# Retention's gates moved behind its keys, values and queries, and its states made among the gates

## The chip, the core and the metric

The kernel runs on one core of a Trainium2 chip. The engines named are PE (TensorE, matmul), DVE (VectorE), ACT (ScalarE), POOL (GpSimd) and SP (SyncE, which here only issues DMAs). The metric is the device time of one execution in microseconds. Before the change three timed runs took 4200.82, 4213.84 and 4215.55 us. One further execution was profiled.

## The reference, cut to what matters

Two blocks of a network follow each other on 1024 tokens of width 1024 (the second block has 256 context tokens as well). The change touches the even layer of the second block, whose mixers are retention and RWKV-7. Both are computed in both directions, for tokens and for context.

```python
u_l = h_l @ w_in                      # also u_c = h_c @ w_in for the context
q, k, v = ret_qkv(u)                  # 8 heads of 64; q and k are rotated for the tokens
gate = silu(u[..., E_RZ:E_WZ])        # and a second gate of 512 columns for RWKV

def retention_scan(q, k, v, log_g, s0):          # chunks of 128 tokens
    scores = einsum('bhncd,bhnsd->bhncs', qc, kc) * dmat       # decay matrix inside a chunk
    y_intra = einsum('bhncs,bhnse->bhnce', scores, vc)
    kv = einsum('bhnsd,bhnse->nbhde', kc * k_decay, vc)
    s_fin, s_prev = lax.scan(lambda s, kv_n: (g_chunk * s + kv_n, s), s0, kv)
    y_cross = einsum('bhncd,nbhde->bhnce', qc * q_decay, s_prev)
    return y_intra + y_cross, s_fin

# forward: context, then tokens from the context's last state; backward: the same on flipped sequences
ret_o = head_rms(ret_fwd + ret_bwd) * gate
y = concat([ret_o, rw_o]) @ w_out
```

`rwkv7_scan` is a recurrence with a state of 64 x 64 for each head; the kernel computes it in chunks of 64 tokens, for which it inverts small triangular matrices.

## The kernel before, in words

The 1280 tokens are ten tiles of 128: tiles 0 to 7 are tokens, 8 and 9 the context. The normalised input lies feature-major in three blocks: block 0 (tiles 0 to 3), block 1 (tiles 4 to 7) and block 2 (the context, 256 columns). Each block and each weight is held as a high part and a low part, and a product takes three matmuls for each of eight slices of the inner dimension, 24 in all (`mm3`, lines 217 to 219). In a profile row, `pf<-whi,hhi` with 128x256 is a projection of keys, values or queries, where weights are the moving side, and `pf<-hhi,whi` is a gate, where the input is moving, with 512 columns for blocks 0 and 1 and 256 for block 2.

A scheduler sets the order of instructions on every engine when the program is built. It takes what is ready in the order of the program text and fills gaps with later work. In the text of `mixers` (line 1488) RWKV comes first and retention behind it. So retention's work serves as filler between RWKV's.

`rwkv` runs ten batches, one chunk pair of the forward and one of the backward direction in each. `prep2` (from line 1580) loads and scales the operands, `invert` (from 1655) inverts on DVE with 31 pairs of a multiply and a reduction (L1670, L1671) and sends the result through DRAM, `merge` (from 1676) reads it back (`wV<-wrd`) and begins with the matmuls of L1694, and `chain` (from 1718) carries the state from chunk to chunk.

Retention in the text before: `ret_proj` is called for block 0, 1 and 2 in turn, and each call does the keys (`rk`), values (`rv`) and queries (`rq`) of the block, six weight tiles, and then its gates (`zT`), eight weight tiles. All results go to DRAM. Block 0 is still in SBUF; blocks 1 and 2 are reloaded (L1508) into the same two buffers of `hA`. Weights are split into high and low for block 0 and read back from DRAM for the others (`whi<-wkh`, `wlo<-wkl`).

`ret_state` stands behind all projections. It loads keys and values of one tile (two buffers), scales the keys on POOL for both directions (L1367), multiplies with values for all eight heads, one matmul of 128x128 by 64 columns each (L1370), and ACT copies the halves into the state array `rS` in SBUF (L1375). Then two chains of nine steps on POOL (L1382, L1383) add up the decayed states, one direction after the other. The decay matrices `rdm` are made on ACT and POOL. `mix_tile` (line 1387) then computes one tile of both mixers' outputs, with states and decay matrices read from SBUF.

Of the kernel before, what the change touches and what calls it, by code (L numbers as in the profile page):

```python
# [10 lines left out]
F32 = mybir.dt.float32  # L11
# [28 lines left out]
class Ker:  # L40
# [995 lines left out]
    def ctx_norm(self):  # L1036
# [227 lines left out]
    def ret_proj(self, p, blocks):  # L1264
# [38 lines left out]

        wc = self.wn // KD
# [15 lines left out]
    def ret_state(self, p, pl):  # L1320
# [3 lines left out]
        lg = p.tile([P, 16], F32, name="rlg")  # L1324
# [3 lines left out]
        tc_ = p.tile([P, 8], F32, name="rtc")  # L1328
        nc.sync.dma_start(tc_, a["c_rtc"])
        qdec = p.tile([P, 8, 2], F32, name="rqdec")  # L1330
        kdec = p.tile([P, 8, 2], F32, name="rkdec")
        gch = p.tile([P, 8], F32, name="rgch")
        for dd in range(2):
            l8 = lg[:, 8 * dd:8 * dd + 8]
            nc.vector.tensor_scalar(qdec[:, :, dd], l8, tc_[:, dd:dd + 1], None, op0=OP.mult)
            nc.vector.tensor_scalar(kdec[:, :, dd], l8, tc_[:, 2 + dd:3 + dd], None, op0=OP.mult)
# [5 lines left out]
        dm = p.tile([P, 8, P], F32, name="rdm")  # L1342
        rel = pl.tile([P, 4, P], F32, name="rrel", tag="rrel", bufs=1)
        nc.sync.dma_start(rel, a["c_rrel"])
        for h in range(8):
            e2 = pl.tile([P, 2, P], F32, name="re2", tag="re2", bufs=2)
# [3 lines left out]
            nc.gpsimd.tensor_add(dm[:, h], e2[:, 0], e2[:, 1])  # L1350

        S_ = p.tile([P, 10, 8, 64], F32, name="rS")
        nc.gpsimd.memset(S_[0:64, 8], 0.0)
        nc.gpsimd.memset(S_[64:128, 9], 0.0)

        nxt = [{8: 9, 9: 0}, {9: 8, 8: 7}]
        for t in range(7):
            nxt[0][t] = t + 1
            nxt[1][t + 1] = t
        for t in [8, 9] + list(range(8)):  # L1360
            k = pl.tile([P, 8, 64], F32, name="rkl", tag="rkl", bufs=2)
            nc.sync.dma_start(k, k_d[t].rearrange("p (h d) -> p h d", d=64))
            v = pl.tile([P, 512], F32, name="rvl", tag="rvl", bufs=2)
            nc.sync.dma_start(v, v_d[t])
            kd = pl.tile([P, 8, 2, 64], F32, name="rkd", tag="rkd", bufs=2)
            for dd in range(2):
                nc.gpsimd.tensor_mul(kd[:, :, dd], k, kdec[:, :, dd:dd + 1].to_broadcast([P, 8, 64]))  # L1367
            ps = self.pf()
            for h in range(8):
                nc.tensor.matmul(ps[:, 64 * h:64 * h + 64], kd[:, h].rearrange("p a d -> p (a d)"),  # L1370
                                 v[:, 64 * h:64 * h + 64], start=True, stop=True)
            for dd in range(2):
                rows = slice(64 * dd, 64 * dd + 64)
                if t in nxt[dd]:
                    nc.scalar.copy(S_[rows, nxt[dd][t]].rearrange("p h d -> p (h d)"), ps[rows])  # L1375
        for dd, t0 in ((0, 8), (1, 9)):
            rows = slice(64 * dd, 64 * dd + 64)
            t = t0
            while t in nxt[dd]:
                n = nxt[dd][t]  # L1380
                tm = pl.tile([P, 8, 64], F32, name="rtm", tag="rtm", bufs=2)
                nc.gpsimd.tensor_mul(tm[rows], S_[rows, t], gch[rows, :, None].to_broadcast([64, 8, 64]))  # L1382
                nc.gpsimd.tensor_add(S_[rows, n], S_[rows, n], tm[rows])  # L1383
                t = n
        self.rt = qdec, dm, S_

    def mix_tile(self, p, pe, t, cat, cv):
# [3 lines left out]
        qdec, dm, S_ = self.rt  # L1391
# [1246 lines left out]
```

## Time and profile before

| what | value |
|---|---|
| timed runs, median | 4213.84 us |
| profiled execution | 4202.26 us, span 4199.8 us |
| mean granted clock of PE | 0.927 of full speed |
| PE busy | 3812.9 us (91%) |
| DVE, ACT, POOL busy | 2130.2, 1320.4, 1129.9 us |
| first and last retention projection | about 2060 us, 2806.6 us |
| last matmul of RWKV | 2926.11 us |
| mix tiles | 2931 to about 3105 us |

The granted clock says how fast PE ran in a stretch: 1.00 is its higher level, 0.50 its lower one. A busy share of PE near 100% says that its stream has work, not which of its work others wait for. For that the chain of waits is read: it follows the work that ended last back from step to step, and gives each piece to an engine and a line.

### The profile page before, as it was taken

What the parts mean: (1) busy time and instruction counts of PE and PEld (TensorE: products, weight loads), DVE (VectorE), ACT (ScalarE), POOL (GpSimd) and SP (SyncE); (2) the same over time, 40 slices, a digit from 0 to 9 for tenths busy, and PEclk for the clock granted to TensorE, in tenths of its full rate; (3) what the DMA queues carried; (4) which work ended last, traced back from release to release, by engine and by line L of the source; (5) the groups of instructions that cost most, each with busy time, mean ns of one, the idle gap of its engine ahead of it and who ended that gap; (6) DMA issues with size and microseconds to landing.
All of it is one profiled execution on the core that took longest, in us unless ns stands there. A gap on an engine that the chain in (4) does not pass through costs nothing. (4 is left out here: it accounts for less than half of the span.)

```text
span 4199.8 us, 59342 instructions
## 1 busy us (share of the span) xinstructions
PE 3812.9 (91%) x23289; PEld 3077.8 (73%) x23289; DVE 2130.2 (51%) x3284; ACT 1320.4 (31%) x2641; POOL 1129.9 (27%) x1153
## 2 busy tenths in 40 slices
PE   7999989988999999789879899887889999998997
PEld 4788877776878788667767687776567877776775
DVE  4232434447343434644337686665556427653576
ACT  4333332215312121442233333332224224332211
POOL 1110202123101011202256343236431200003674
PEclk8999979998999999988989999876899999998998
DMA  5321227573141413333477655653754644324465
GB/s 201 123 100 67 98 84 264 189 263 118 50 148 63 147 50 129 126 125 122 138 229 221 187 161 173 206 157 99 234 188 142 225 134 125 102 70 152 165 203 193
DMA packets 453574, 627.03 MB, mean 149 GB/s; under 512 B 142577, under 2 KB 302499, under 8 KB 447152
## 3 DMA queue, kind: packets, MB, share of 16 engines
q1 hardware_dynamic: 402816, 421.50, 31.1%
q0 software_dynamic: 50480, 201.75, 14.5%
q8 instruction: 184, 3.01, 0.3%
q14 instruction: 94, 0.77, 0.1%
HBM read 427.27 MB, written 195.19 MB: 148 GB/s over the span
## 5 line engine op out<-in xcount | busy, mean ns | idle before, releaser
L217 PE MATMUL p<-hhi,whi 128*128 128x512 f32 x1056 | 415.8, 394 | 5.9 <-DVE hf L389 5.8
L218 PE MATMUL p<-hlo,whi 128*128 128x512 f32 x1056 | 414.3, 392 | 4.3 <-DVE hlo L391 4.3
L219 PE MATMUL p<-hhi,wlo 128*128 128x512 f32 x1056 | 413.8, 392 | 0.0
L217 PE MATMUL pf<-whi,hhi 128*128 128x512 f32 (+1 forms) x992 | 359.0, 362 | 29.4 <-ACT rqr L1279 9.4
L218 PE MATMUL pf<-wlo,hhi 128*128 128x512 f32 (+1 forms) x992 | 352.4, 356 | 3.7 <-DVE wlo L177 3.4
L177 DVE TENSOR_TENSOR wlo<-wraw,whi 128x2048 fp32r<-128x2048 f32 (+1 forms) x103 | 212.3, 2062 | 273.8 <-ACT whi L176 267.8
L219 PE MATMUL pf<-whi,hlo 128*128 128x512 f32 (+1 forms) x992 | 349.3, 353 | 0.0
L176 ACT CAST whi<-wraw 128x2048 fp32r<-128x2048 f32 (+1 forms) x123 | 193.2, 1575 | 459.6 <-PE pt L219 174.7
L217 PE MATMUL pf<-hhi,whi 128*128 128x512 f32 (+1 forms) x640 | 252.4, 394 | 6.0 <-DVE zt L1311 2.1
L218 PE MATMUL pf<-hlo,whi 128*128 128x512 f32 (+1 forms) x640 | 252.0, 394 | 0.0
L219 PE MATMUL pf<-hhi,wlo 128*128 128x512 f32 (+1 forms) x640 | 249.4, 390 | 0.0
L217 PEld LDWEIGHTS pf<-whi,hhi 128*128 128x128 f32 x992 | 198.7, 200 | 68.2 <-issue 14.1
L217 PE MATMUL pj<-whi,hhi 128*128 128x512 f32 (+1 forms) x560 | 216.5, 389 | 26.5 <-ACT whi L176 12.1
L217 PEld LDWEIGHTS p<-hhi,whi 128*128 128x128 f32 x1056 | 200.4, 190 | 54.1 <-DVE hf L389 6.2
L218 PEld LDWEIGHTS p<-hlo,whi 128*128 128x128 f32 x1056 | 200.2, 190 | 46.3 <-DVE hlo L391 5.3
L219 PEld LDWEIGHTS p<-hhi,wlo 128*128 128x128 f32 x1056 | 200.0, 189 | 42.6 <-issue 0.8
L218 PEld LDWEIGHTS pf<-wlo,hhi 128*128 128x128 f32 x992 | 198.9, 200 | 28.9 <-issue 4.1
L219 PE MATMUL pj<-whi,hlo 128*128 128x512 f32 (+1 forms) x560 | 214.1, 383 | 3.0 <-DVE hlo L381 3.0
L218 PE MATMUL pj<-wlo,hhi 128*128 128x512 f32 (+1 forms) x560 | 215.1, 384 | 0.2 <-DVE wlo L177 0.2
L219 PEld LDWEIGHTS pf<-whi,hlo 128*128 128x128 f32 x992 | 198.5, 200 | 22.1 <-issue 1.3
L1670 DVE TENSOR_TENSOR wtm<-wT,wL 128x2 f32<-128x2 f32 (+30 forms) x310 | 145.7, 470 | 37.5 <-POOL wL L1661 28.0
L217 PEld LDWEIGHTS pf<-hhi,whi 128*128 128x128 f32 x640 | 122.9, 192 | 37.9 <-issue 6.7
(750 smaller groups left out, 8544.6 us busy)
## 6 DMA issues: line engine op xcount, KB each, us to landing
wraw<-w_in POOLq DMA_DIRECT2D x25, 1024.0 KB, 6.0
wraw<-w_ada POOLq DMA_DIRECT2D x24, 1024.0 KB, 8.5
wraw<-w_up POOLq DMA_DIRECT2D x22, 1024.0 KB, 6.0
whi<-wkh POOLq DMA_DIRECT2D x40, 512.0 KB, 5.6
wlo<-wkl POOLq DMA_DIRECT2D x40, 512.0 KB, 5.2
wraw<-ada_w POOLq DMA_DIRECT2D x32, 512.0 KB, 4.5
ox<-x SPq DMA_DIRECT2D x48, 256.0 KB
xp<-xl SPq DMA_DIRECT2D x48, 256.0 KB
```

Of the source, the lines that this page charges most:

```text
L176: nc.scalar.copy(hi[:, :n], raw[:, :n])
L177: self.we.tensor_sub(lo[:, :n], raw[:, :n], hi[:, :n].bitcast(F32))
L217: mm(out, L[0], R[0], start=first, stop=False)
L218: mm(out, L[0], R[1], start=False, stop=False)
L219: mm(out, L[1], R[0], start=False, stop=last)
L1670: nc.vector.tensor_mul(tv, T[:, r0:, i:], L[:, i:i + 1, i:].to_broadcast([P, 16 - r0, n]))
```

## The change

Three things are changed. First, keys, values and queries of all three blocks come first, and the gates of all blocks behind them, in the order of blocks 2, 1, 0. Block 2 is still in SBUF then, and blocks 1 and 0 are reloaded, so block 0 is now stored as well (line 1048). Second, the states are made step by step beside the gates: a generator does one step for each gate of a block and is run out at the end. A step takes four heads and both directions at once, the forward direction in partitions 0 to 63 and the backward one in 64 to 127, each at its own tile. Its keys and values have one buffer each; the sum with the decayed state is done by DVE from PSUM. Every state goes to DRAM. Third, the decay matrices go to DRAM too, and the mix tiles load states and matrices from there.

```diff
-        for b in (1, 2):
+        for b in range(3):
             hT = self.nT[b]
             self.nT_d[b] = [self.dr.tile(list(t.shape), F32, name=f"nTd{b}{x}") for t, x in zip(hT, "hl")]
...
+    def ret_gates(self, p, blocks):
...
         for c0 in range(0, 1024, wc):
             W = self.wcols_kept(self.kept, w, 1536 + c0, wc)
             for c in range(0, wc, P):
-                self.proj_fm(self.nT, W, c, ev_z((c0 + c) // P), blocks)
+                for b in blocks:
+                    self.proj_fm(self.nT, W, c, ev_z((c0 + c) // P), [b])
+                    yield
...
+        order = ([8, 9] + list(range(8)), [9, 8] + list(range(7, -1, -1)))
+        for g in range(2):
+            S_ = pl.tile([P, 4, 64], F32, name="rS", tag="rS", bufs=2)
+            nc.gpsimd.memset(S_, 0.0)
+            for n in range(10):
+                for dd in range(2):
+                    rows = slice(64 * dd, 64 * dd + 64)
+                    nc.sync.dma_start(self.st_d[order[dd][n]][rows, g], S_[rows].rearrange("p h d -> p (h d)"))
+                if n == 9:
+                    break
+                k = pl.tile([P, 2, 4, 64], F32, name="rkl", tag="rkl", bufs=1)
+                v = pl.tile([P, 2, 256], F32, name="rvl", tag="rvl", bufs=1)
+                for x, x_d in ((k.rearrange("p a h d -> p a (h d)"), k_d), (v, v_d)):
+                    for dd in range(2):
+                        nc.sync.dma_start(x[:, dd], x_d[order[dd][n]][:, 256 * g:256 * g + 256])
+                nc.gpsimd.tensor_mul(k, k, kdec[:, :, 4 * g:4 * g + 4, None].to_broadcast([P, 2, 4, 64]))
+                ps = self.pf()
+                for h in range(4):
+                    for dd in range(2):
+                        nc.tensor.matmul(ps[64 * dd:64 * dd + 64, 64 * h:64 * h + 64], k[:, dd, h],
+                                         v[:, dd, 64 * h:64 * h + 64], start=True, stop=True, tile_position=(0, 64 * dd))
+                tm = pl.tile([P, 4, 64], F32, name="rtm", tag="rtm", bufs=1)
+                nc.gpsimd.tensor_mul(tm, S_, gch[:, 4 * g:4 * g + 4, None].to_broadcast([P, 4, 64]))
+                S_ = pl.tile([P, 4, 64], F32, name="rS", tag="rS", bufs=2)
+                nc.vector.tensor_add(S_, tm, ps[:, :256].rearrange("p (h d) -> p h d", d=64))
+                yield
...
+            dm = pl.tile([P, P], F32, name="rdm", tag="rtm", bufs=1)
+            nc.gpsimd.tensor_add(dm, e2[:, 0], e2[:, 1])
+            nc.sync.dma_start(self.dm_d[:, h], dm)
...
+        S_ = p.tile([P, 8, 64], F32, name="rSl", tag="rSl", bufs=3)
+        nc.sync.dma_start(S_, self.st_d[t].rearrange("p g (h d) -> p (g h) d", d=64))
...
+            with self.pool("rpb") as pb:
+                self.ret_tables(pb)
+                for b in range(3):
+                    if b:
+                        block(b)
+                    self.ret_proj(pb, [b])
+
+            with self.pool("rzb") as pb, self.pool("rsl") as pl:
+                steps = self.ret_state(pl)
+                for b in (2, 1, 0):
+                    if b < 2:
+                        block(b)
+                    for _ in self.ret_gates(pb, [b]):
+                        next(steps, None)
+                self.run(steps)
```

Here `block(b)` reloads block b into the two buffers of `hA`. The order of the built programs shows what the scheduler makes of it. On PE, where RWKV ends, before: the last four groups are of `chain`, and the mix stage (`colr`, `wraw`, `rql`) follows at once.

```order
L1746 MATMUL p_20019<-wxv,wam 64x64 x8
L1753 MATMUL p_20019<-wrs,wX_1_13941 64x64 x8
L1779 MATMUL p_20019<-wS,wrr 64x64 x8
L1784 MATMUL p_20019<-wxv,wam 64x64 x8
L405 MATMUL pf<-ident,colr 128x8
L282 MATMUL pa<-wraw,cT_7260 32x512 x2
L1409 MATMUL pf<-ident,rql 128x128 x4
```

On PE at the same place after the change (lines of `chain` are 16 higher there): the last two groups of `chain` stand between gates.

```order
L219 MATMUL pf<-hhi,wlo 128x512
L217 MATMUL pf<-hhi,whi 128x512
L1795 MATMUL p_20020<-wS,wrr 64x64 x8
L1800 MATMUL p_20020<-wxv,wam 64x64 x8
L218 MATMUL pf<-hlo,whi 128x512
L219 MATMUL pf<-hhi,wlo 128x512
L217 MATMUL pf<-hhi,whi 128x512
```

Behind the last group of `chain` 98 matmuls of gates stand before the mix stage begins. Next, SP's queue at the last merges, before: the inversion is stored (`wrd`) and read back (`wV`), one load of values for the states (`rvl`) follows, and loads and stores of `chain`.

```order
L1674 DMA wrd_13966<-wT 1024x1x32 x2
L1686 DMA wV<-wrd_13966 32x8x32 x8
L1364 DMA rvl<-rv_13887 128x512
L1714 DMA wxv<-rw_vt_12036 64x4x64
L1715 DMA wxv<-rw_vt_12036 64x4x64
L1788 DMA rwy_6_13913<-wyt 128x256
L1714 DMA wxv<-rw_vt_12037 64x4x64
```

SP's queue at the last merges after the change: `rst` are the stores of states, `rvl` and `rkl` the loads of a step, `nTd0h` and `nTd0l` the reload of block 0.

```order
L1702 DMA wV<-wrd_13967 32x8x32 x3
L1804 DMA rwy_1_13919<-wyt 128x256
L1702 DMA wV<-wrd_13967 32x8x32 x5
L1730 DMA wxv<-rw_vt_12041 64x4x64
L1731 DMA wxv<-rw_vt_12041 64x4x64
L1315 DMA zT<-zt 128x512
L1359 DMA rst_22265<-rS 64x256
L1359 DMA rst_22264<-rS 64x256
L1366 DMA rvl<-rv_13888 128x256
L1366 DMA rvl<-rv_13887 128x256
L1512 DMA hhi<-nTd0h 128x4096
L1512 DMA hlo<-nTd0l 128x4096
```

Stores and loads of the states, and the reload of block 0, now stand in SP's queue between RWKV's own loads. Two loads of keys stand directly ahead of these rows, between the store of the inversion and its first read.

## Rows read from the trace of the kernel before

**Rows 1.** By stretch: length, busy PE, PEld, DVE, ACT, POOL, PEclk, DMA share, GB/s.

```profile
2236.70:2299.40 62.70, 59.26 (x618) 49.28 (x618) 50.02 (x104) 22.79 (x51) 41.73 (x54) 0.90 0.73 223
2299.40:2383.90 84.50, 72.67 (x798) 59.40 (x797) 58.95 (x117) 31.89 (x77) 32.61 (x40) 0.92 0.67 216
2383.90:2456.50 72.60, 66.15 (x798) 57.83 (x797) 54.11 (x116) 28.02 (x76) 34.62 (x65) 0.98 0.52 147
2456.50:2524.90 68.40, 63.31 (x766) 56.72 (x765) 50.30 (x110) 26.11 (x71) 28.18 (x49) 0.90 0.57 168
2524.90:2590.20 65.30, 61.05 (x670) 50.69 (x671) 52.15 (x115) 22.19 (x58) 28.02 (x52) 0.97 0.58 163
2590.20:2677.60 87.40, 74.26 (x802) 62.44 (x801) 52.47 (x114) 30.02 (x78) 21.61 (x38) 0.90 0.65 200
2677.60:2759.00 81.40, 64.29 (x779) 57.22 (x779) 49.81 (x112) 27.84 (x74) 23.36 (x41) 0.89 0.74 219
2759.00:2825.70 66.70, 60.40 (x695) 53.15 (x696) 53.96 (x122) 26.41 (x75) 26.61 (x40) 0.78 0.45 133
2825.70:2900.20 74.50, 57.29 (x541) 53.35 (x540) 50.04 (x98) 21.85 (x50) 55.70 (x60) 0.50 0.32 82
2900.20:2927.20 27.00, 19.36 (x482) 16.88 (x480) 12.62 (x22) 9.59 (x26) 14.50 (x15) 0.88 0.19 55
2927.20:2950.00 22.80, 17.02 (x123) 11.62 (x121) 7.23 (x14) 8.69 (x17) 10.41 (x11) 0.81 0.97 306
```

**Rows 2.** The chain of waits from 2236 to 2900 us, its share by line.

```profile
by line: DVE wtm L1670 11.7%; DVE wT L1671 7.6%; DMA wV<-wrd 5.8%; DMA wlt<-wam 5.2%; PE pf L217 4.9%; issue 4.7%; PE pf L218 4.5%; PE pf L219 4.3%; PE pj L1642 3.4%; DMA wrd<-wT 3.4%; DVE wam L1644 3.2%; DVE wxv L1738 2.9%; DVE wt L1772 2.
```

**Rows 3.** PE's timeline: start and length in us; two gate matmuls, five steps apart.

```profile
2352.12 0.39 PE L217 MATMUL pf<-hhi,whi 128*128 128x512 f32 x1
...
2353.28 0.39 PE L219 MATMUL pf<-hhi,wlo 128*128 128x512 f32 x1
```

**Rows 4.** Timelines at the reload of block 1: SP's issue, PE's first uses of each half.

```profile
2353.70 0.34 SPq L1508 DMA_DIRECT2D hhi<-nTd1h  x1
...
2362.48 0.36 PE L217 MATMUL pf<-whi,hhi 128*128 128x256 f32 x1
...
2371.73 0.56 PE L219 MATMUL pf<-whi,hlo 128*128 128x256 f32 x1
```

**Rows 5.** PE's timeline in the last batch of RWKV and at its end.

```profile
2905.52 0.69 PE L1784 MATMUL p<-wxv,wam 128*64 128x64 f32 x16
2906.13 0.69 PE L1701 MATMUL p<-wX,wQ 32*32 32x32 f32 x32
...
2931.04 0.24 PE L405 MATMUL pf<-ident,colr 8*128 8x8 f32 x1 [3.81 <-DMA colr<-rw_ln_b]
```

**Rows 6.** Busy time by stretch, of the states' matmuls (L1370) alone.

```profile
2806.60:2900.20 93.60, 36.96 (x160) 34.95 (x160) 0.52 0.34 88
```

**Rows 7.** Four lines of POOL and one of DVE: shortest, median, longest in ns.

```profile
L1367 POOL TENSOR_TENSOR rkd<-rkl,rkdec x20: 1040/1048/1375, 2818.4 to 2881.8; 128x512 f32<-128x512 f32 x20
L1382 POOL TENSOR_TENSOR rtm<-rS,rgch x18: 1034/1041/1324, 2813.3 to 2910.5; 64x512 f32<-64x512 f32 x18
L1383 POOL TENSOR_TENSOR rS<-rS,rtm x18: 1254/1262/1521, 2837.9 to 2911.6; 64x512 f32<-64x512 f32 x18
L1739 POOL TENSOR_TENSOR wS<-wt,wfc x38: 607/648/1049, 2261.2 to 2920.7; 128x256 f32<-128x256 f32 x38
L1772 DVE TENSOR_TENSOR wt<-p,wS x76: 403/422/430, 2259.3 to 2920.1; 64x256 f32<-64x256 f32 x76
```

**Rows 8.** Busy time by stretch, of the inversion's multiplies (L1670) alone.

```profile
2695.00:2738.00 43.00, 10.80 (x31) 1.00 0.65 202
...
2839.00:2878.00 39.00, 22.61 (x31) 0.50 0.29 88
```

**Rows 9.** Waits of SP's queue, 2806 to 2900 us: total, times, longest.

```profile
SPq L1362 <- POOL rkd L1367: 16.8, 7, 3.7
...
SPq L1364 <- PE pf L1370: 9.5, 5, 6.2
```

More of the change, by code (lines that the diff above doesn't have):

```diff
@@ L1341, in ret_state @@
         nc.vector.tensor_scalar(kdec, kdec, 0.125, None, op0=OP.mult)
-        dm = p.tile([P, 8, P], F32, name="rdm")
-        rel = pl.tile([P, 4, P], F32, name="rrel", tag="rrel", bufs=1)
+        self.st_d = [self.dr.tile([P, 2, 256], F32, name=f"rst{t}") for t in range(10)]
+        self.dm_d = self.dr.tile([P, 8, P], F32, name="rdmd")
+        order = ([8, 9] + list(range(8)), [9, 8] + list(range(7, -1, -1)))
[24 more added lines that the diff above has]
+                yield
+        rel = pl.tile([P, 4, P], F32, name="rrel", tag="rkl", bufs=1)
         nc.sync.dma_start(rel, a["c_rrel"])
         for h in range(8):
-            e2 = pl.tile([P, 2, P], F32, name="re2", tag="re2", bufs=2)
+            e2 = pl.tile([P, 2, P], F32, name="re2", tag="rS", bufs=2)
             for dd in range(2):
@@ L1349, in ret_state @@
             nc.gpsimd.tensor_mul(e2, e2, rel[:, 2:4])
[L1350 to L1385, printed above, removed]
+            dm = pl.tile([P, P], F32, name="rdm", tag="rtm", bufs=1)
+            nc.gpsimd.tensor_add(dm, e2[:, 0], e2[:, 1])
+            nc.sync.dma_start(self.dm_d[:, h], dm)
+        self.qdec = qdec
     def mix_tile(self, p, pe, t, cat, cv):
         nc = self.nc
-        qdec, dm, S_ = self.rt
+        qdec, dm = self.qdec, self.dm
         py = lambda: self.ps.tile([P, 512], F32, name="py", tag="py", bufs=2)
@@ L1430, in mix_tile @@
             nc.tensor.matmul(o, sD[:, h % 2, h // 2], v[:, 64 * h:64 * h + 64], start=True, stop=False)
-            nc.tensor.matmul(o, qdT[:, h], S_[:, t, h], start=False, stop=True)
+            nc.tensor.matmul(o, qdT[:, h], S_[:, h], start=False, stop=True)
         cols = slice(t * P, t * P + P)
@@ L1494, in mixers @@
         self.open_ps(2)
-        with self.pool("rwm") as p, self.pool("rpb") as pb:
+        with self.pool("rwm") as p:
             self.rwkv(p)
@@ L1499, in mixers, with block @@
             self.we = self.nc.gpsimd
-            self.ret_tables(pb)
             self.kept = {}
-            for b in range(3):
-                if b:
-                    n = 512 if b < 2 else 256
-                    hT = tuple(self.hA.tile([P, KD, 512], F32R, name="h" + x, tag=f"h{x}", bufs=1)[:, :, :n]
-                               for x in ("hi", "lo"))
-                    for t, src in zip(hT, self.nT_d[b]):
-                        self.nc.sync.dma_start(t.bitcast(F32), src)
-                    self.nT[b] = hT
-                self.ret_proj(pb, [b])
+            def block(b):
+                n = 512 if b < 2 else 256
+                hT = tuple(self.hA.tile([P, KD, 512], F32R, name="h" + x, tag=f"h{x}", bufs=1)[:, :, :n]
+                           for x in ("hi", "lo"))
+                for t, src in zip(hT, self.nT_d[b]):
+                    self.nc.sync.dma_start(t.bitcast(F32), src)
+                self.nT[b] = hT
+            with self.pool("rpb") as pb:
[12 more added lines that the diff above has]
+                self.run(steps)
             self.close_all("wp", "hA")
-            ers = ExitStack()
-            rst = ers.enter_context(self.pool("rst", side=self.ms))
-            with self.pool("rsl", side=self.ms) as pl:
-                self.ret_state(rst, pl)
         self.ms, self.ss = "left", "right"
@@ L1520, in mixers @@
         self.open_ps(2, 1)
-        with ers, self.pool("ret") as pr:
+        with self.pool("ret") as pr:
             self.open_hA()
@@ L1525, in mixers @@
             cat = [self.alloc_hT(b) for b in range(3)]
+            self.dm = pr.tile([P, 8, P], F32, name="rdml")
+            self.nc.sync.dma_start(self.dm, self.dm_d)
             with self.pool("eop") as pe:
```

15 lines of the change are left out of this document (8 added, 7 removed).

## The prediction

> **What bounds the kernel now.** The change lies in the even layer's mixers, 2060 to 3105 us of a span of 4199.8 us; the profiled execution took 4202.26 us, the median of the three timed runs is 4213.84. I read first the table of busy time by stretch, one stretch for each of the ten batches of the RWKV recurrence, cut at the first matmul of a batch's merges [rows 1]. In eight of the nine full periods PE is busy 79 to 95% of the time, because projections of retention (keys, values, queries, gates) stand in its stream between the matmuls of RWKV. In the ninth, 2825.7 to 2900.2, they are used up: PE works at a granted clock of 0.50 (its lower level), POOL is busy 55.70 of 74.5 us with retention's states, and the period is no shorter than the others. Then come 27.0 us of RWKV alone, and the mix tiles, where DMA stands at 0.97 at first.
>
> Second, the chain of waits over the nine periods [rows 2]: no engine holds it. The inversion on DVE (L1670, L1671) has 19.3%, DRAM trips of RWKV's own data some 14%, and the three lines of retention's projections (L217 to L219) 13.7%, which is 91 of 663.5 us. So the reader is to see two things: PE is full, but it is full of filler, and the filler is the limit for a small part only. Third, lengths: the four periods with neither states nor a reload of the normalised input (62.7, 72.6, 68.4, 65.3 us) have a mean of 67.3; the other periods up to 2759, in or behind a reload, have 81.4 to 87.4.
>
> **The change part by part.** The order of instructions says what moves. Between the first and the last merges 959 matmuls of keys, values and queries stand in both kernels, and 192 gate matmuls of 256 columns in both. Of the 384 gate matmuls of 512 columns 191 are left there; 193, all gates of block 0, now stand behind the last merges, 98 of them behind the last matmul of RWKV, where before there was none.
>
> Tail. A gate matmul of 512 columns takes 0.232 us at full clock, five steps in 1.16 us [rows 3]; 193 take 44.8. They need block 0 again, a reload of two times 2 MB. A like reload was issued at 2353.70, its first half was used at 2362.48 and its second at 2371.73 [rows 4], so it takes between 9 and 18 us; 4.2 MB at the 306 GB/s of the stretch behind 2927.2 [rows 1] is 14, which I take. It can be issued some 6 us behind the first merge (an estimate: two groups of merges and the evacuation of block 1's last gate). RWKV's matmuls that stand among block 0's gates are 128 in the order, 16 groups, and the three last state steps are 3 more; groups of this size stand 0.61 us apart in the last batch at full clock [rows 5], so 12 us. Together 6 + 14 + 45 + 12 = 77 us, where RWKV alone took 27.0 [rows 1]. The pause from 2927.2 to the mix stage at 2931.04 [rows 5] stays: the loads of the first tile stand on SP behind the last gate's store, as they now stand behind RWKV's last. Term: +50.
>
> Periods. They lose the same 44.8 us of PE work. If PE were the limit, all of it would come back; if only what the chain books to the projections counts, 91 us of some 223 (959 + 192 of 256 columns at half of 0.232, 384 whole), 41% or 18 us does. I take one half, since a shorter PE queue also ends some waits that are booked to ACT and DVE: -22, bounds 0 and -45.
>
> States out of the ninth period. 160 matmuls of 36.96 us at clock 0.52 go [rows 6], and 144 with half the columns of weights come. The period is 7 us above the mean of 67.3; -7, bounds 0 and -37.
>
> States beside gates. Eighteen steps now lie among gates and RWKV. DVE gets 18 additions from PSUM, 128x256, like L1772 at 0.42 us [rows 7]: 7.6 us. POOL loses the 20 + 18 + 18 operations of L1367, L1382, L1383 (62.4 us) and gets 18 of 1.05 and 18 of 0.65 (like L1739): 30.5 us [rows 7]. The rows show what POOL's work does to the inversion: 31 multiplies took 10.80 us at 2695 to 2738, and 22.61 us in the ninth period, where POOL worked on states [rows 8]. That is 11.8 us for some 29 us of POOL (55.70 of 74.5, over 39 us), 0.4 for one; 30.5 us then cost 12, with the additions 20 us of DVE, of which I count half, as DVE has some half of the chain: +10. Bounds: 0, and 47 by the queue rival below.
>
> The Trainium skill ("GPSIMD Engine Reference", Key points) says that GpSimd shares its SBUF interfaces with VectorE and contends with VectorE instructions that have two SBUF inputs. L1670 is such an instruction and L1671, with one, is not, so the trace agrees in kind. Taken to the full, a microsecond of VectorE for each of GpSimd, it would make this term about 19 and the time 4258; the rows say 0.4, and the sum goes by them.
>
> Reloads. Within the nine periods there are three instead of two, on SP among RWKV's own loads: 14 us of DMA, hidden while RWKV works, but the periods in or behind a reload are 14 to 20 us longer than 67.3. Not all of that can be the reload's; +3, bounds 0 and +20. The new store of block 0 (4.2 MB near 1810 us, in a stage of dense projections) I count as nothing, since no result waits for it; without that cover it is 14 us at 306 GB/s.
>
> Mix tiles. Each loads 256 KB of state, and the decay matrices come back from DRAM, 3.1 MB or 10 us at 306 GB/s, in a stage with a DMA share of 0.97 at first and room later; +1, bounds 0 and +10.
>
> Sum: 50 - 22 - 7 + 10 + 3 + 1 = +35 us. On the profiled execution that is 4237; on the median, 11.6 us above it, 4249. The latter I predict.
>
> **Rivals.**
> PE is the limit after all (the other side, faster). For it: PE at 91 to 95% in five of the nine periods, and the ninth at half clock. Against it: the period with the most filler, 2524.9 to 2590.2, is among the shortest. Then the nine periods give back the whole 45, the states another 25 of their 37 (18 groups of 0.64 us remain), nothing is lost to additions or reloads, and the reload of block 0 takes 9: 45 - 45 - 25 + 1 = -24 on the median, 4190. It decides from the point where the mean period falls from 73.7 to below 68, since 50 / 9 is 5.6.
>
> Half way: the 45 come back whole, all other terms stand: 50 - 45 - 7 + 10 + 3 + 1 = +12, 4226, no change that can be told.
>
> SP's queue becomes the limit. SP issues in order. In the ninth period's states its loads waited 16.8 + 9.5 us for 20 issues [rows 9], with two buffers; now 72 loads with one buffer each and 40 stores stand among RWKV's loads of merges and values, each ready only when a step's matmuls or addition are done. By that ratio SP waits 95 us; half of it on the chain is 47 instead of 10: 4286. Against it: the steps stand far apart in the order.
>
> **How the numbers follow.** Forecast 0.38, PE limit 0.20, half way 0.25, queue 0.17. A change below 0.5% (21 us, 4193 to 4235) is about what can't be told from none. Faster is most of the PE rival: 0.18. Same is the half-way case and the edge of that one: 0.27. Slower is the forecast and the queue: 0.55. The forecast's own range is 4235 to 4268. The whole range reaches to 4188, where about half of the PE rival is left out, and to 4305, the queue rival with a full 18 us reload and some more.
>
> **What would show it.** Right: gates with PE nearly full from some 15 to 25 us behind the last merges, for about 55 us, and RWKV's last matmul 20 us before the end of that; nine periods with a mean of 70 to 72; state additions in the middle of the inversion; no stretch at clock 0.50 as long as the ninth period. Wrong: a mean period under 68 (PE rival), SP waits of the state loads of over 60 us (queue rival), or gates in the tail at the low clock, which would add up to 45 us.

## The result, and the profile after

The changed kernel takes 4258.08 us (median of four runs, 4242.59 to 4278.92); the kernel before, run beside it, 4210.68. The ratio is 1.0121, with a 95% interval of 1.0099 to 1.0143: slower by 47 us between the medians, where 35 on the median of the runs had been predicted, 4249. The profiled execution took 4260.93 us with a span of 4259.1, 59.3 more than the span before. The two profiles lie further apart than the medians, since the profiled execution of the kernel before was 8 us under its median.

Busy time of the changed kernel by stretch (columns as in [rows 1]): nine periods, each from the first merges of a batch to the next; the last merges to the last gate; the pause; the mix stage, from the first transposes of queries to the first matmul of the output projection.

```profile
2240.40:2296.30 55.90, 52.33 (x604) 46.50 (x604) 45.87 (x97) 17.01 (x45) 31.93 (x53) 0.76 0.69 229
2296.30:2380.90 84.60, 74.88 (x849) 65.27 (x848) 56.96 (x123) 33.19 (x89) 40.40 (x73) 0.86 0.48 137
2380.90:2439.20 58.30, 52.41 (x717) 46.61 (x716) 47.05 (x108) 20.73 (x57) 19.06 (x33) 0.97 0.55 160
2439.20:2509.00 69.80, 60.09 (x700) 52.07 (x698) 53.29 (x110) 25.52 (x68) 33.26 (x61) 0.80 0.59 173
2509.00:2583.30 74.30, 66.95 (x736) 59.18 (x736) 49.52 (x114) 25.33 (x67) 20.50 (x36) 0.82 0.64 188
2583.30:2671.30 88.00, 64.66 (x737) 56.37 (x736) 57.21 (x115) 29.75 (x76) 31.39 (x38) 0.78 0.61 176
2671.30:2751.50 80.20, 67.54 (x737) 57.93 (x737) 59.28 (x123) 28.38 (x69) 33.52 (x38) 0.69 0.65 186
2751.50:2829.20 77.70, 69.12 (x727) 55.66 (x726) 55.56 (x119) 25.84 (x67) 24.04 (x38) 0.84 0.58 183
2829.20:2883.50 54.30, 43.65 (x559) 35.20 (x559) 39.19 (x99) 10.54 (x26) 14.05 (x23) 0.84 0.66 185
2883.50:2966.20 82.70, 73.07 (x710) 57.84 (x706) 19.29 (x39) 19.86 (x51) 24.18 (x40) 0.86 0.67 226
2966.20:2973.80 7.60, 0.12 (x1) 0.03 (x1) 0.76 (x2) 0.60 (x1) 0.00 (x0) 0.83 0.49 167
2973.80:3172.00 198.20, 166.81 (x1132) 119.75 (x1132) 108.09 (x178) 50.86 (x92) 85.35 (x92) 0.76 0.68 220
```

And the mix stage of the kernel before, in the same columns:

```profile
2933.10:3113.10 180.00, 146.53 (x1130) 102.26 (x1128) 104.64 (x179) 50.91 (x92) 88.62 (x92) 0.83 0.72 226
```

The difference of 59.3 us is laid out by landmarks. The first merges stand at 2240.4 instead of 2236.7: +3.7. The nine periods take 643.1 us instead of 663.5: -20.4. From the last merges to the last PE work of RWKV or gates it is 82.7 instead of 27.0: +55.7. From there to the mix stage 7.6 instead of 5.9: +1.7. The mix stage takes 198.2 instead of 180.0: +18.2. What comes behind it, 1087 us, differs by 0.4.

The chain of waits over the nine periods, by line, against [rows 2]:

```profile
by line: DVE wtm L1686 11.3%; DVE wT L1687 7.2%; PE pj L1658 6.4%; DVE wbk L1636 5.0%; DMA wlt<-wam 4.9%; issue 4.8%; DMA wV<-wrd 3.8%; DMA wL<-wlt 3.4%; PE pf L217 3.4%; PE pf L218 3.0%; DVE wxv L1754 2.9%; PE pf L219 2.8%; DVE wam L1660 2
```

The filler (L217 to L219) falls from 13.7 to 9.2% of the chain, from 91 to 59 us. Of these 32 us only 20 came back: other links took their place, such as matmuls of `prep2` (L1642 before, L1658 after), from 3.4 to 6.4%.

The tail, from PE's and SP's timelines of the changed kernel (start, length in us):

```profile
2884.14 0.50 PE L219 MATMUL pf<-hhi,wlo 128*128 128x512 f32 x1
...
2888.77 0.83 SPq L1512 DMA_DIRECT2D hhi<-nTd0h  x1
...
2898.70 0.77 PE L217 MATMUL pf<-hhi,whi 128*128 128x512 f32 x1 [1.31 <-DMA hhi<-nTd0h]
...
2904.86 0.80 PE L218 MATMUL pf<-hlo,whi 128*128 128x512 f32 x1 [0.33 <-DMA hlo<-nTd0l]
...
2936.74 0.69 PE L1800 MATMUL p<-wxv,wam 128*64 128x64 f32 x16
...
2965.78 0.39 PE L219 MATMUL pf<-hhi,wlo 128*128 128x512 f32 x1
...
2969.61 0.32 SPq L1541 DMA_DIRECT2D rdml<-rdmd  x1
2969.98 0.42 SPq L1397 DMA_DIRECT2D rql<-rq  x1
...
2973.81 1.12 PE L1414 MATMUL pf<-ident,rql 128*128 128x128 f32 x4 [7.49 <-DMA rql<-rq]
```

Read from top to bottom: block 1's last gate ends and frees the buffer; SP issues the reload of block 0; its halves are used 10 and 16 us later; from then on gates stand dense; RWKV is done at 2937.4, and 28.8 us of gates follow. The mix stage starts only when SP has passed the reload of the decay matrices and the loads of the first tile have landed.

### The profile page after: what moved, and what is told of

Same layout as the page of the kernel before. It is cut to its first block, busy times and chain, and to the rows that moved or that the text cites. A ratio compares the mean times of both kernels' runs of the same rounds, so it can differ in the third digit from the quotient of the medians.

```text
span 4259.1 us, 59783 instructions
## 1 busy us (share of the span) xinstructions
PE 3864.9 (91%) x23417; PEld 3118.3 (73%) x23417; DVE 2133.1 (50%) x3302; ACT 1310.1 (31%) x2623; POOL 1094.0 (26%) x1133
## 4 chain that ended last, share of the span: by engine, by line
PE 25%; DVE 9%; DMA 6%; issue 5%; POOL 3%; SPq 1%; ACT 1%; POOLq 0%; DVEq 0%; ACTq 0%
PE pf L217 2%; PE pf L218 2%; PE pf L219 2%; PE pj L217 2%; PE pj L218 2%; PE pj L219 2%; DVE wtm L1686 2%; PE pj L1658 1%; DVE wT L1687 1%; PE p L2107 1%; DMA wlt<-wam 1%; DVE wbk L1636 1%; PE pa L282 1%; PE pj L2447 1%; PE p L2095 1%
## 5 line engine op out<-in xcount | busy, mean ns | idle before, releaser
L217 PE MATMUL p<-hhi,whi 128*128 128x512 f32 x1056 | 416.4, 395 | 5.8 <-DVE hf L389 5.7
L219 PE MATMUL p<-hhi,wlo 128*128 128x512 f32 x1056 | 414.3, 393 | 0.0
L217 PE MATMUL pf<-whi,hhi 128*128 128x512 f32 (+1 forms) x992 | 360.6, 364 | 16.2 <-ACT rqr L1279 7.1
L219 PE MATMUL pf<-whi,hlo 128*128 128x512 f32 (+1 forms) x992 | 350.6, 354 | 0.0
L217 PE MATMUL pf<-hhi,whi 128*128 128x512 f32 (+1 forms) x640 | 257.3, 402 | 8.5 <-DVE zt L1314 2.2
L219 PE MATMUL pf<-hhi,wlo 128*128 128x512 f32 (+1 forms) x640 | 251.7, 393 | 1.6 <-DMA wlo<-wkl 1.6
L217 PEld LDWEIGHTS pf<-whi,hhi 128*128 128x128 f32 x992 | 199.9, 202 | 56.5 <-ACT th L542 9.2
L217 PEld LDWEIGHTS p<-hhi,whi 128*128 128x128 f32 x1056 | 200.7, 190 | 54.0 <-DVE hf L389 6.1
L217 PE MATMUL pj<-whi,hhi 128*128 128x512 f32 (+1 forms) x560 | 216.5, 389 | 24.0 <-ACT whi L176 10.5
L219 PEld LDWEIGHTS p<-hhi,wlo 128*128 128x128 f32 x1056 | 200.2, 190 | 42.9 <-issue 0.8
L218 PEld LDWEIGHTS pf<-wlo,hhi 128*128 128x128 f32 x992 | 200.7, 202 | 32.9 <-issue 5.6
L219 PEld LDWEIGHTS pf<-whi,hlo 128*128 128x128 f32 x992 | 199.9, 202 | 22.8 <-issue 2.1
L219 PE MATMUL pj<-whi,hlo 128*128 128x512 f32 (+1 forms) x560 | 213.8, 383 | 2.7 <-DVE hlo L381 2.7
L1686 DVE TENSOR_TENSOR wtm<-wT,wL 128x2 f32<-128x2 f32 (+30 forms) x310 | 143.8, 464 | 41.8 <-POOL wL L1677 32.6
L217 PEld LDWEIGHTS pf<-hhi,whi 128*128 128x128 f32 x640 | 125.6, 196 | 41.2 <-issue 8.8
```

What stands on the lines that cost most here:

```text
L217: mm(out, L[0], R[0], start=first, stop=False)
L218: mm(out, L[0], R[1], start=False, stop=False)
L219: mm(out, L[1], R[0], start=False, stop=last)
L1686: nc.vector.tensor_mul(tv, T[:, r0:, i:], L[:, i:i + 1, i:].to_broadcast([P, 16 - r0, n]))
```

## The experiments

In the table are, from each profile, us from the first merges of the first period to the last merges, from there to the mix stage, the mix stage with PE's mean granted clock, and the point at which the mix stage ends. "Gates behind" are gate matmuls of 512 columns behind the last merges in the order of instructions. Times are medians; the ratio to the kernel before has its interval, where several rounds were run.

| kernel | time | ratio | gates behind | nine periods | to the mix | mix stage, clock | its end |
|---|---|---|---|---|---|---|---|
| before | 4210.7 | 1 | 0 | 663.5 | 32.9 | 180.0, 0.83 | 3113.1 |
| before, again | 4199.4 (one run) | | 0 | 657.3 | 35.5 | 183.7, 0.84 | 3113.4 |
| changed | 4258.1 | 1.0121 (1.0099 to 1.0143) | 193 | 643.1 | 90.3 | 198.2, 0.76 | 3172.0 |
| changed, again a | 4259.9 | 1.0127 (1.0110 to 1.0144) | 193 | 640.2 | 94.1 | 187.7, 0.80 | 3164.9 |
| changed, again b | 4258.1 (one run) | | 193 | 643.5 | 88.6 | 194.9, 0.75 | 3167.9 |
| block 0's gates at home | 4230.8 | 1.0071 (1.0048 to 1.0093) | 25 | 653.3 | 78.3 | 178.1, 0.77 | 3145.5 |
| all gates at home | 4243.8 | 1.0095 (1.0073 to 1.0116) | 0 | 646.4 | 112.8 | 143.3, 0.90 | 3143.5 |
| no state steps | 4215.0 | 1.0025 (1.0008 to 1.0042) | 162 | 640.5 | 65.1 | 177.4, 0.88 | 3124.4 |
| one state for all tiles | 4245.3 | 1.0102 (1.0077 to 1.0127) | 193 | 640.3 | 83.8 | 186.2, 0.83 | 3153.6 |
| decay matrices first | 4229.1 | 1.0053 (1.0037 to 1.0070) | 127 | 661.8 | 57.7 | 165.4, 0.91 | 3133.7 |
| the same, block 0's gates at home | 4227.6 | 1.0050 (1.0033 to 1.0067) | 48 | 654.1 | 51.5 | 196.9, 0.80 | 3141.0 |
| the same, all gates at home, steps from block 2's queries on | 4231.6 | 1.0057 (1.0045 to 1.0070) | 0 | 646.7 | 72.5 | 180.3, 0.83 | 3142.0 |
| changed, 30 more matmuls in the mix stage | 4257.6 | 1.0119 (1.0098 to 1.0140) | 193 | 641.3 | 97.5 | 191.1, 0.91 | 3171.5 |

**Block 0's gates at home.** A part undone: these gates stand behind block 0's own projections again.

```diff
                     self.ret_proj(pb, [b])
+                    if not b:
+                        for _ in self.ret_gates(pb, [b]):
+                            pass
...
-                for b in (2, 1, 0):
+                for b in (2, 1):
```

> Block 0's gates stand directly behind block 0's keys, values and queries again (no reload of block 0); block 1's and block 2's gates and the states stay as in the changed kernel. In the order of instructions 25 gate matmuls stand behind the last merges instead of 193. Tail theory (the cost is the gates behind the last merges): the stretch from the last merges to the last filler falls from 82.7 us to some 35 (-48), and the nine periods, which take 168 gates of 0.232 us back, grow by half of these 39 us (+20): 4258 - 28 = 4230. State theory (the cost is the scheme of the states, DRAM trips on SP's queue and more loads in the mix stage, all of it still there): within 10 us of 4258. PE-limit theory (what is put back into the periods costs its whole 39): 4249.

It took 4230.8, the number of the tail theory, but not in its way. RWKV and gates end 42.8 us behind the last merges, 40 us sooner than in the changed kernel (48 were expected), but the mix stage begins 35.5 us later still, so the stretch to it is only 12 us shorter. The other gains are the mix stage (16 us under the mean of the three profiles of the changed kernel) and earlier first merges (6), against 11 us of longer periods, where 20 were expected. SP's and PE's timelines of this kernel:

```profile
2925.84 7.96 SPq L1387 DMA_DIRECT2D rdmd<-rdm  x4
...
2930.82 1.12 PE L1803 MATMUL p<-wxv,wam 128*64 128x64 f32 x16
...
2957.57 0.39 SPq L1387 DMA_DIRECT2D rdmd<-rdm  x1
2962.59 0.32 SPq L1544 DMA_DIRECT2D rdml<-rdmd  x1
2962.96 0.42 SPq L1397 DMA_DIRECT2D rql<-rq  x1
...
2967.41 1.12 PE L1414 MATMUL pf<-ident,rql 128*128 128x128 f32 x4 [3.25 <-DMA rql<-rq]
```

The eight decay matrices are made behind the last state step, one after the other through one buffer (L1387 stores it); their reload (L1544) waits for the last store, with the first tile's loads behind it on SP. Ahead of the last two stores SP also waits with loads of the mix stage (L1444):

```profile
SPq L1444 <- DVE erp_e L154: 8.6, 2, 5.5
...
SPq L1544 <- DMA rdmd<-rdm: 4.6, 1, 4.6
```

So behind the gates there stands a second late chain: the states, then the decay matrices, then their reload. In the changed kernel its last store is issued at 2956.59, and the gates, until 2966.2, cover it.

**All gates at home.** Only the new states are left of the change.

```diff
                     self.ret_proj(pb, [b])
+                    if b < 2:
+                        for _ in self.ret_gates(pb, [b]):
+                            pass
...
-                for b in (2, 1, 0):
-                    if b < 2:
-                        block(b)
-                    for _ in self.ret_gates(pb, [b]):
-                        next(steps, None)
+                for _ in self.ret_gates(pb, [2]):
+                    next(steps, None)
```

> All gates stand behind their own block's projections, as in the kernel before; only the new states remain of the change, beside block 2's gates. In the order no gate stands behind the last merges, but 80 state matmuls (10 steps), 40 of them behind RWKV's last matmul. Tail theory: the last stretch is 27 us of RWKV and some 5 steps of about 4 us behind it, 47 in place of 82.7 (-36), the periods take the 45 us of gates back at half (+22): 4258 - 14 = 4244. State theory: no faster than the changed kernel, since the steps at the end have nothing beside them and the loads in the mix stage stay: 4258 to 4275.

4243.8, the number of the tail theory again, but neither of its parts. The matmuls of the last step end at 2958.8, 71 us behind the last merges (47 expected), and the periods are 4 us longer than in the changed kernel, not 22. The second chain is now fully bare: the mix stage begins at 3000.2. It lasts only 143.3 us there because part of its work that needs neither states nor matrices ran in the gap. With no gate behind the merges this kernel is still 0.95% slower than the one before: the states and decay matrices at the end cost by themselves.

**No state steps.** The 18 steps are left out, and the states stored are zero.

```diff
-                if n == 9:
-                    break
+                if n % 9 == 0 or n > 0:
+                    continue
```

> The changed kernel with the 18 state steps left out (no loads of keys and values, no multiplies, matmuls or additions for them; the states stored are all zero, so that part of the result is missing). 162 gates stand behind the last merges instead of 193. Tail theory: the steps cost the +10 us of the prediction's coupling term, and 31 gates fewer in the tail are 7 us, half of it paid in the periods: 4258 - 14 = 4244; a tail of some 70 us stays. State theory (steps on POOL, DVE and SP hold the recurrence): -47, 4211, the whole difference to the kernel before.

4215.0: the tail theory's 4244 is missed, the state theory's 4211 met. Its mechanism is not: the nine periods take 640.5 us without the steps and 640.2 to 643.5 with them, and the run without them has 31 gates more in its periods, 7 us of PE. So in this order the steps lengthen the periods by some 7 us at most, not by 47. What changed is the tail. Without steps 31 gates more stand ahead of the last merges, and the reload of block 0 with them:

```profile
2854.05 0.32 SPq L1512 DMA_DIRECT2D hlo<-nTd0l  x1
2854.46 0.38 SPq L1512 DMA_DIRECT2D hhi<-nTd0h  x1
```

That is 28 us ahead of the last merges (2881.9), where the changed kernel issues it 5 us behind them (2888.77). The stretch to the mix stage is 25 us shorter: 7 for 31 gates, most of the rest the reload that nobody waits for now. A third thing moved with them: with no steps ahead of them the decay matrices are made early, too, and their last store is issued at 2756.72, where the changed kernel issues it at 2956.59:

```profile
2756.72 0.39 SPq L1387 DMA_DIRECT2D rdmd<-rdm  x1
```

So this run takes the second chain out of the tail as well, and doesn't tell what the steps alone cost. The mix stage is 10 to 21 us shorter than in the three profiles of the changed kernel.

**One state for all mix tiles.** Nine loads of 256 KB are left out.

```diff
-        S_ = p.tile([P, 8, 64], F32, name="rSl", tag="rSl", bufs=3)
-        nc.sync.dma_start(S_, self.st_d[t].rearrange("p g (h d) -> p (g h) d", d=64))
+        if t == 8:
+            self.s1 = p.tile([P, 8, 64], F32, name="rSl", tag="rSl", bufs=1)
+            nc.sync.dma_start(self.s1, self.st_d[t].rearrange("p g (h d) -> p (g h) d", d=64))
+        S_ = self.s1
```

> The changed kernel, where the ten mix tiles all use one state loaded once (nine loads of 256 KB left out; the result is that of the wrong states). The order up to the mix stage is the same. From the mix stage's first transposes to its load of the output weights the changed kernel takes 190.6 us, the kernel before 172.6. Clock theory (the stage is longer because the granted clock is low for longer, by chance or by the pause ahead of it, not by its loads): the time stays within 6 us of 4258, and the stage's length goes with its granted clock. Load theory (the states' loads hold the stage): -9 x 256 KB at 306 GB/s or more, -8 to -18: 4240 to 4250.

4245.3: the number is the load theory's, and the clock theory's 4252 or more is missed. But the ratio's interval overlaps those of the changed kernel, so alone it decides nothing. 6.5 us of it is an earlier start of the stage; the stage, 186.2 us, is within 2 us of a profile of the changed kernel with all loads.

**Decay matrices first.** The core of the edit; the tables of decay go to constants, and the matrices get buffers of their own, two for the result.

```diff
                     self.ret_proj(pb, [b])
+                    if not b:
+                        with self.pool("rdc") as pl:
+                            self.ret_state(pl)
...
-                steps = self.ret_state(pl)
+                steps = self.ret_steps(pl)
```

> The changed kernel with the decay matrices (and the tables of decay they and the steps use) computed and stored behind block 0's projections instead of behind the last state step; everything else as in the changed kernel. In the order 127 gate matmuls stand behind the last merges (193 in the changed kernel) and none behind RWKV's last. Chain theory (states, then eight decay matrices one after the other through one buffer and DRAM, then their reload ahead of the first mix tile on SP, set the start of the mix stage as much as the gates do): the stretch from the last merges to the mix stage falls from 90.3 us to some 50, and the periods take 66 gates at half their 15 us: 4258 - 32 = 4226. Gates theory (only the gates behind the merges count): 66 x 0.232 = 15 us less there, 8 back in the periods: 4251.

4229.1, where the chain theory said 4226. The same gates, steps and loads, with one group of small operations moved ahead in the text, and 29 us are gone. The scheduler's order moved with it: 66 gates fewer stand behind the last merges, and block 0's reload is issued 43 us ahead of them, at 2867.14. Of the end of the mix stage (3133.7 against a mean of 3168.3 in three profiles of the changed kernel) the stretch to the mix stage gives 33, the stage itself 28, and the later first merges (7) and longer periods (20) take 27 back. The last gate is now done before RWKV is. So the chain theory's number was met by luck in part: the stretch fell to 57.7 us, not to 50, the periods grew by 20 us and not by 8, and the 28 us of the stage were in neither theory. The 20 us are more than the 15 that 66 gates take at full clock; where the rest arises was not traced.

**The same with block 0's gates at home, or all.** Beside the move of the decay matrices, the first has the edit of block 0's gates above; the second has block 0's and 1's gates at home and starts the steps earlier:

```diff
...
+                steps = self.ret_steps(pl)
+                for base in self.ret_proj(pb, [2]):
+                    if not base:
+                        next(steps, None)
+                for _ in self.ret_gates(pb, [2]):
+                    next(steps, None)
+                    next(steps, None)
```

> The kernel with block 0's gates at home (4230.8 measured) and the decay matrices moved ahead as in the run beside it, behind block 0's gates. In its trace without that move RWKV ended at 2931.9 and the mix stage began at 2967.4, 35 us later, behind the last decay matrix. Chain theory: this falls to about 6 us, 48 instead of 25 gates behind the last merges cost 5: 4231 - 24 = 4207, the time of the kernel before. Gates theory: the decay matrices are hidden, only the 23 gates count: 4236.

> All gates at home (4243.8 measured), the decay matrices moved ahead, and the state steps begun beside the queries of block 2 instead of beside its gates, two steps for each gate. In the order 8 of the 18 steps stand behind the last merges, 5 behind RWKV's last matmul, with 72 gate matmuls of 256 columns. Chain theory: 27 us of RWKV, 5 steps of 5 us, 6 us to the mix stage and its 178 make 236 from the last merges to the output projection, where the kernel with all gates at home took 256: 4244 - 20 = 4224. Gates theory: no gate of 512 columns stands behind the merges in either, so no change: 4244.

4227.6 and 4231.6: the chain theory asked for 4207 and 4224, the gates theory for 4236 and 4244. In the first the mix stage begins 7.8 us behind RWKV's end as expected, 27 us sooner after the last merges than without the move, but its end is only 8 us sooner after them: it runs at a clock of 0.80, and the work that had filled the gap is in it again. Both theories are too simple there; what the stage itself takes counts as much as when it starts. No version was as fast as the kernel before, and none pointed to one that would be.

**The changed kernel and the one before, again.** No edit.

> The changed kernel once more, unchanged. Its mix stage (first transposes of queries to the first matmul of the output projection) took 198.2 us at a mean granted clock of 0.76; over the other kernels it took 165.4 at 0.91, 177 to 180 at 0.83 to 0.88, 186 at 0.83 and 196.9 at 0.80. Chance theory (the same instructions meet a different granted clock from run to run): this profile differs from 198.2 by 10 us or more, with its clock; the stretch from the last merges to the mix stage stays within 3 us of 90.3. Fixed theory (the changed order enters the stage so that it always runs low): 194 to 202 at 0.74 to 0.78. Time 4258 within 6 us.

> The same as the run beside it: chance theory, a mix stage that differs by 10 us or more from one of the other two profiles of this kernel; fixed theory, 194 to 202 us.

> The kernel before once more, unchanged: its mix stage took 180.1 us at a granted clock of 0.83. Chance theory: it may differ by 10 us or more from that; fixed theory: 177 to 183. The tail behind the last merges stays at 27 us.

The mix stage of the changed kernel, a second and a third time (columns as above):

```profile
2977.20:3164.90 187.70, 158.59 (x1133) 111.62 (x1133) 105.22 (x179) 50.87 (x92) 86.76 (x92) 0.80 0.72 232
```

```profile
2973.00:3167.90 194.90, 165.54 (x1132) 117.88 (x1132) 103.99 (x178) 50.84 (x92) 86.76 (x92) 0.75 0.70 223
```

Both theories hold in part. The same program's stage varies by 10.5 us with its clock, but its three profiles (mean 193.6) all lie above the two of the kernel before (mean 181.9). So some 12 us of the 18 seem to belong to the kernel and the rest to the one profile, as far as three profiles against two can tell.

**More matmuls in the mix stage.** Three are added to each tile, ahead of other matmuls.

```diff
+        def warm():
+            w = self.ps.tile([P, 512], F32, name="pw", tag="pw", bufs=1)
+            nc.tensor.matmul(w, self.ident, dm[:, 0:4].rearrange("p a n -> p (a n)"), start=True, stop=True)
...
+        warm()
```

> The changed kernel with 30 matmuls of 128x512 added in the mix stage (three for each tile, into a PSUM bank that nobody reads), so that TensorE has work where it waits. By the stage's own rows (32-row matmuls of 512 columns at 0.75 us) they are some 25 to 30 us of work, of which the idle 31 us of the stage can hold a part. Clock theory (the stage's length hangs on the granted clock, which falls behind stretches where the engine waits): the granted clock rises from 0.76 to 0.85 or more, the stage falls to some 180 or less: 4240. Work theory: the clock stays where it is and the added work costs its half: 4258 + 13 = 4271.

The stage, and in it the added matmuls alone (PE and PEld; each matmul is two instructions):

```profile
2980.40:3171.50 191.10, 171.05 (x1192) 112.99 (x1190) 107.28 (x179) 52.00 (x92) 87.53 (x91) 0.91 0.71 225
2980.40:3171.50 191.10, 32.86 (x59) 9.23 (x58) 0.91 0.71 225
```

Neither forecast: the clock rose to 0.91 as the clock theory wanted, and the time stayed at 4257.6. PE is busy with the added matmuls for 32.9 us, a part of it overlapped by their neighbours, which leaves at least 138 us for its other work, where that took 159 to 167. So at the higher clock the stage's own PE work was up to some 20 to 29 us shorter, and the added work took as much.

## Why the prediction was right, and where not

**Tail, +50: right, +55.7.** 20 us were taken until the gates stand dense, 21.4 were measured (5.3 to the reload's issue, 16.1 for the reload with 14 taken). RWKV's last matmul ends 28.8 us before the last gate; 20 had been named. The last 61.3 us hold 44.8 of gates by the price taken, and 16.5 of RWKV's groups, state steps and 3.6 us of waits for gate weights, with 12 taken; the clock there was 0.96, so the low clock that had been named as a sign of being wrong did not come. The experiments say more of this term: with 25 gates behind the merges the stretch to the end of RWKV and gates is 42.8 us, with 127 it is 50.0, with 162 and no steps 56.9, none of them with a reload in it, and with 193 and the reload 82.7. So 127 gates, 29.5 us, made it 23 us longer than the 27.0 of RWKV alone. The other 32.7 us are about the 15.3 of 66 more gates and the 16.1 from the reload's issue to the use of its second half.

**The period terms, -22 - 7 + 10 + 3 = -16: right in sum, -20.4, but by luck in its parts.** The mean period is 71.5 us; 70 to 72 had been said. The PE rival needed 68 or less, so it is out. The half-way rival named 4226 and is out by the time. But the ninth period is 54.3 us instead of 74.5, which is -20.2 where -7 was taken, inside the bound of -37; the other eight give -0.2 together, as the fifth (+9) and the eighth (+11) ate what the first and third gave. The half that was taken for the gates is not borne out: 288 gate matmuls of 512 columns, 66.8 us by the price taken, left the eight periods, 95 of them into the ninth, and the eight are no shorter. By stretch, the kernel before, the changed kernel, and the one with all gates at home:

```profile
2236.70:2825.70 589.00, 521.39 (x5914) 446.73 (x5915) 421.76 (x905) 215.25 (x555) 236.74 (x376) 0.91 0.62 186
```

```profile
2240.40:2829.20 588.80, 507.99 (x5798) 439.59 (x5798) 424.72 (x905) 205.75 (x537) 234.10 (x368) 0.81 0.60 177
```

```profile
2241.00:2820.10 579.10, 504.63 (x5776) 429.38 (x5777) 419.06 (x901) 209.55 (x535) 229.83 (x363) 0.91 0.61 183
```

PE's busy time fell by 13.4 us only, and the granted clock from 0.91 to 0.81: with less filler PE is busy for 86% of the eight periods instead of 89, and what is left runs slower. Over all versions the clock of these eight periods goes with the number of 512-column gates in them: 0.90 to 0.92 with 384 (four profiles), 0.87 with 240, 0.85 with 216, 0.83 with 132, 0.81 to 0.84 with 96 (five profiles), 0.82 with 57. The prediction priced the periods at one clock and left this out. How much of their length hangs on the clock was not tested.

The queue rival is out by its own sign:

```profile
SPq L1366 <- PE pf L1371: 33.1, 9, 10.5
...
SPq L1366 <- DMA wlba<-rw_ba: 2.3, 1, 2.3
...
SPq L1366 <- DMA rkl<-rk: 1.3, 1, 1.3
```

These waits of the state loads, over the stretch with steps, are 37 us in the changed kernel, where 60 were named; and without any steps the periods are no shorter than with them.

**States beside gates, +10: the contention is there, but its size was misread, and the consequence was not seen.** Over the four last periods the inversion's multiplies (L1686, alone, by stretch) take 59.96 us with steps, in the changed kernel, and 54.16 in the one without:

```profile
2583.30:2883.50 300.20, 59.96 (x124) 0.78 0.62 182
```

```profile
2593.90:2881.90 288.00, 54.16 (x124) 0.80 0.62 187
```

That is 5.8 us, with POOL busy 103.0 and 88.3 us in them, 0.39 per microsecond of POOL, where 0.4 was taken. The agreement is luck. The 0.4 divided by all of POOL's time in the ninth period, as if POOL had been idle in the stretch it was compared with; by the rows POOL was busy 14.35 us there and 30.39 in the ninth period, which makes 11.8 / 16.0 = 0.74, and the term 15 instead of 10:

```profile
2695.00:2738.00 43.00, 40.20 (x521) 36.06 (x521) 36.98 (x91) 15.90 (x44) 14.35 (x26) 1.00 0.65 202
2839.00:2878.00 39.00, 29.86 (x234) 28.13 (x234) 36.45 (x68) 7.81 (x17) 30.39 (x29) 0.50 0.29 88
```

Nor is there one factor: over the same four periods the multiplies take 65.00 us with POOL at 101.3 in the run with one state, and 57.33 with POOL at 112.8 in the one with the decay matrices first. Their length goes with the time in which POOL works beside them, which is, from the trace, 20.6 us without steps, 25.7 with the decay matrices first, 28.4 in the changed kernel and 33.8 with one state; POOL's busy time does not give that. The Trainium skill ("GPSIMD Engine Reference", Key points) has contention between GpSimd and VectorE instructions with two SBUF inputs; the trace agrees in kind, as the reductions (L1687), with one input, take 42.35 us in both kernels.

The larger price of the steps is not a longer period. With them the scheduler put 31 gates, the reload of block 0 and the decay matrices behind the last merges, and the run without steps, where all three are gone from there, shows a stretch 25 us shorter.

**The pause stays: nearly, +1.7, but its reason was not the one given.** The first loads stand on SP behind the last gate's store, and also behind the reload of the decay matrices. That chain would have let the reload go some 8 us sooner (its last store is issued at 2956.59, and with block 0's gates at home the reload came 5.0 us behind the last store; here it came at 2969.61). The prediction counted these matrices as a transfer in the mix stage and left out that they are made last. It cost nothing here, as the gates were later; it is why, with block 0's gates at home, the stretch to the mix stage fell by 12 us and not by the 40 by which RWKV and gates were done sooner.

**Mix tiles, +1: this is the step that failed.** It measured +18.2 in the profiled pair, 11.7 in the means of three and two profiles, outside its bounds of 0 to 10. It was sized by the loads alone, and the loads do not make the stage long by themselves: with all of them, and the decay matrices first, the stage takes 165.4 us, less than before the change:

```profile
2968.30:3133.70 165.40, 140.33 (x1134) 100.17 (x1133) 105.15 (x180) 50.61 (x92) 83.77 (x88) 0.91 0.77 250
```

The same 1130 or so matmuls take PE 140 us there and 167 in the changed kernel, at 0.91 and 0.76 of the clock. The order of this stage's instructions is not fixed either: the scheduler writes it anew for each kernel. Why the changed kernel's order and start meet the lower clock stays open. It is shown that the stage is not long wherever the loads are, and that it varies by 10 us for one program; a share of some 7 us for the loads in the changed kernel's own order is not excluded (186.2 us with one load against the mean of 193.6).

**The store of block 0, 0:** the first merges came 3.7 us later in the profiled pair, 4.6 in the means. Where these arise was not traced.

The sum: 3.7 - 20.4 + 55.7 + 1.7 + 18.2 + 0.4 = 59.3 against 35. The direction was right, and so was the main mechanism of this kernel's tail: filler, with a reload ahead of it, now stands behind the work it used to fill. Of the 24 us missing in the profiled pair, 17 are the mix stage; between the medians 12 are missing. What the sum didn't have is that the gates at the end need not cost much: the run without steps has 162 of them there and is 0.25% slower than the kernel before, though it lacks the states' work as well. Of the 47 us, 29 go once the decay matrices are made first, which also takes the reload out of the tail; the rest is not parted here between the steps, the periods and the mix stage.

## What to carry to other kernels

Filler that is moved to the end of a recurrence is paid there, beyond the holes that it can still fill, and the periods that it leaves need not give it back: here 44.8 us of gates and the states went, and 20.4 us came back, all of it in the period that the states had held. Taking filler away can lower the granted clock of what stays, so a price at full clock promises too much. Before pricing a tail, list everything that is emitted late and ends there (states, small tables, a reload, a queue's order), since a chain that is hidden today is the limit once the first one goes. And a change of order early in a scheduled program also rewrites the order of stages behind it, so their length needs a range of its own.

## What the runs showed of the hardware

One stage with the same matmuls ran at mean granted clocks from 0.75 to 0.91 and took 165 to 198 us, and one unchanged program differed by 10.5 us in it from run to run. One fall came behind waits of PE: in the kernel before, PE was busy 5.62 of the 10 us from 2971 and had the lower level, 0.50, for the next 10, in which it was busy throughout:

```profile
2971.00:2981.00 10.00, 5.62 (x30) 3.54 (x30) 9.54 (x15) 2.01 (x5) 4.51 (x5) 0.79 0.45 148
2981.00:2991.00 10.00, 10.00 (x68) 8.45 (x66) 2.54 (x4) 1.64 (x2) 3.28 (x3) 0.50 0.51 155
```

Not expected: matmuls that nobody needs, 32.9 us of PE's busy time, left the time as it was (4257.6 us against 4258.1), beside a granted clock of 0.91 where three profiles without them had 0.75 to 0.80. And the first eight periods, with 66.8 us less of filler, ran at 0.81 to 0.83 in three profiles, where they had run at 0.91 and 0.92 in two, and were no shorter.
